# An SSD layer's turnings in one step, and TensorE's order tied once per chunk

## The chip, the cores and the metric

The kernel runs on one core of a Trainium2 chip. The metric is device time in microseconds (us) of one execution; the kernel before took 1810.02 us in the median of three runs (1809.37 to 1811.35). The core's engines are TensorE (PE in the profile, PEld for its weight loads), VectorE (DVE), ScalarE (ACT), GpSimd (POOL) and SyncE (SP, which issues most of the DMAs).

## The reference

Two layers over 256 context rows and 1024 latent rows of width 1024. Layer 0 is gated windowed attention, layer 1 a gated bidirectional Mamba-2 SSD mixer, and a final RMSNorm follows. The change touches layer 1 alone. Cut to it:

```python
z, xbc, dt_raw = jnp.split(h @ w_in, [SSD_WIDTH, SSD_WIDTH + SSD_CONV_DIM], axis=-1)
xbc = jax.nn.silu(centred_depthwise_conv(xbc, conv_w, conv_b))       # 5 taps
xs, bm, cm = jnp.split(xbc, [SSD_WIDTH, SSD_WIDTH + SSD_GROUPS * SSD_STATE], axis=-1)
# per direction, over chunks of 128 rows, per group g (8), head r (4 a group), width 64, state 128
states = jnp.einsum('bcsgn,bcsgr,bcsgrp->bcgrpn', bm, decay_to_end, xdt)
h = exp(a_last) * h + states                                         # scan over the chunks
cb = jnp.einsum('bcqgn,bcsgn->bcqsg', cm, bm)
y_diag = jnp.einsum('bcqsg,bcqsgr,bcsgrp->bcqgrp', cb, lmat, xdt)
y_off = jnp.einsum('bcqgn,bcgrpn,bcqgr->bcqgrp', cm, h_prev, jnp.exp(a_cs))
u = (y_f + y_b + d_skip * xs) * jax.nn.silu(z)                       # forward and backward
out = (rms_normalize(u) * norm_w) @ w_out
```

## The kernel before, in words

**Groups and chunks.** Layer 1 works group by group (8 groups, one for every 256 columns of the mixer). A group needs four projected tiles of 128 channels (B in `bT`, two x tiles in `cacc`, C in `cT`) and the gate z. Each product is split in three (high by high, high by low, low by high). `front(g)` is a generator that gives out the projections of group g one matmul at a time, with an estimated cost each: 24 matmuls of 256 columns for the context (L1085, into the PSUM tile `psD`, of which there is one buffer), 48 of 512 columns for the latent rows (L1095, into `pj2`, two buffers), and for z 192 of 256 columns (L1129, into `pj2` too). After a tile's projections ScalarE takes the first tap (L1007), VectorE the other four (L1011), then the silu (L1018, L1019).

**Turnings.** B and x are needed with rows on the partitions too. `natural` (L1053) turns a tile back in blocks of 128 columns: TensorE writes the turned blocks over the projection's own PSUM tile (L1058), and ScalarE copies them out (L1061): two copies of 512 columns for the latent rows, one of 256 for the context, which sits in `psD`. These steps go to a queue, `post`, with a delay (`LATE`), and are recorded when the estimated cost given out has passed it.

**The scan.** `slot` is one chunk of one group: it opens with the matmul of C and B (`pcb`, L1247), the two products with the states (`po`, L1249 with the forward state, L1250 with the backward one), then the step of the forward state (`S`, L1256), the product within the chunk (`yd`, four matmuls at L1281) and, for the chunk before, the turning of the result (`tail`, two at L1312). These five PSUM tiles share `psX`, three buffers. VectorE, GpSimd and ScalarE make the decay matrix, the sums and the norm between them. `states` runs the chain of backward states of the next group, one link at a time (L1198, into the same `psD` as the context's projections): GpSimd weights x (L1173, `xw`) and decays the state (L1178), VectorE adds (L1210).

**How they are woven.** While group g is scanned, `slot` calls `fill(0)` to `fill(4)` between its parts; each draws projections of group g+1 (in the last group: the output projection, `ssd_out`, L1527) from the generator up to a share of the total, and runs `post` for what was given out; `tick` draws a link of `states`. So the code's order is fixed by estimated costs. It is not yet the engines' order: the framework's scheduler lays the recorded instructions out again, engine by engine, by priority in the order of recording and by when it reckons their inputs and buffers ready. An engine then works its list strictly in order, and a matmul that waits holds up those behind it. In the scheduled order of before, projections stand between the opening's parts, and turnings stand in fours. The second four of a tile (L1058) wait for the copy of the first four (L1061).

## Time and profile before

| | us |
|---|---|
| median of three runs | 1810.02 |
| the profiled execution, its own time | 1807.02 |
| its span, first to last instruction | 1805.3 |
| TensorE matmul busy | 1739.6 (96%) |
| VectorE / ScalarE / GpSimd busy | 1181.8 / 867.1 / 799.0 |
| first opening of a chunk (L1247) to the last | 849.3 to 1674.8 |
| time from a group's first opening to the next group's, groups 1 to 2 | 105.8 |

The page gives each engine's busy time and the costliest groups of instructions with the idle time ahead of them and what ended it ("<-"). A timeline lists instructions by start; "x4" are four merged ones, and the bracket behind a row is the engine's idle time before it. An fp32 matmul that is not a turning leaves two records. Rows of a stretch ("A:B") give the busy time of PE, PEld, DVE, ACT and POOL with the number of instructions, the granted TensorE clock, and the DMA's share and rate.

### The profile page before, as it was taken

How to read it: one execution, taken by the hardware profiler on the slowest of the kernel's cores; microseconds unless marked ns; L12 is line 12 of the kernel's file. 1: busy time of each engine (PE TensorE's matmuls, PEld its weight loads, DVE VectorE, ACT ScalarE, POOL GpSimd, SP SyncE). 2: the span in 40 equal slices, each digit the busy share in tenths (PEclk: the TensorE clock that was granted, in tenths of full speed). 3: DMA queues.
4: the chain of work that ended last, by engine and by line, in shares of the span. 5: the costliest groups of instructions: out<-in, count | busy, mean ns of one | idle time of the engine just before them, and what ended most of it. 6: DMA issues, size and time to landing. Idle time of an engine off the chain costs nothing.

```text
span 1805.3 us, 28983 instructions
## 1 busy us (share of the span) xinstructions
PE 1739.6 (96%) x10319; PEld 1494.7 (83%) x10319; DVE 1181.8 (65%) x2115; ACT 867.1 (48%) x1906; POOL 799.0 (44%) x1068
## 2 busy tenths in 40 slices
PE   6899999999999999999999999999999999999997
PEld 2697788888888887778888898988889898888887
DVE  4634436778877885684776858577684867766734
ACT  3612237777777774452443525344353534544522
POOL 2331127555575545103454544645454464554411
PEclk9999999999999999999999999999999999999999
DMA  9558856444455436222222323222332322656533
GB/s 334 226 144 268 283 177 149 106 100 111 111 153 130 120 102 221 73 53 73 71 77 82 92 62 98 79 71 79 81 93 62 100 73 76 174 169 170 175 101 121
DMA packets 212495, 227.61 MB, mean 126 GB/s; under 512 B 16384, under 2 KB 149632, under 8 KB 212352
## 3 DMA queue, kind: packets, MB, share of 16 engines
q1 hardware_dynamic: 178288, 207.12, 38.0%
q0 software_dynamic: 34064, 18.65, 5.8%
q8 instruction: 81, 1.33, 0.3%
q14 instruction: 62, 0.51, 0.1%
HBM read 190.88 MB, written 35.13 MB: 125 GB/s over the span
## 4 chain that ended last, share of the span: by engine, by line
PE 81%; DVE 9%; ACT 4%; DMA 3%; issue 2%; SPq 1%; POOL 1%; DVEq 0%; ACTq 0%; POOLq 0%
PE pj L1095 17%; PE pj L1129 10%; PE pj L1527 7%; PE pj L246 6%; PE pj L247 6%; PE pj L248 6%; PE psD L1085 4%; PE psX L1281 3%; PE pt L684 3%; PE psD L1198 2%; PE pv L691 2%; PE pv L690 1%; PE S L659 1%; PE S L658 1%; PE psX L1249 1%
## 5 line engine op out<-in xcount | busy, mean ns | idle before, releaser
L246 PE MATMUL pj<-uH,wh 128*128 128x512 f32 (+1 forms) x712 | 257.4, 363 | 9.0 <-ACT uH L470 6.3
L247 PE MATMUL pj<-uL,wh 128*128 128x512 f32 (+1 forms) x712 | 243.3, 342 | 0.5 <-POOL uL L707 0.4
L248 PE MATMUL pj<-uH,wl 128*128 128x512 f32 (+1 forms) x712 | 242.4, 341 | 1.4 <-POOL wl L231 1.4
L1095 PE MATMUL pj<-uH,wl 128*128 128x512 f32 x512 | 172.7, 405 | 0.0
L1095 PE MATMUL pj<-uH,wh 128*128 128x512 f32 x512 | 171.4, 405 | 1.2 <-ACT bn L1061 0.7
L1095 PE MATMUL pj<-uL,wh 128*128 128x512 f32 x512 | 169.2, 402 | 0.0
L246 PEld LDWEIGHTS pj<-uH,wh 128*128 128x128 f32 x712 | 135.6, 191 | 36.2 <-ACT uH L470 7.7
L1129 PE MATMUL pj<-wh,uH 128*128 128x256 f32 x512 | 150.3, 294 | 9.1 <-ACT xn L1061 9.1
L1173 POOL TENSOR_TENSOR xw<-xn,dtdec 128x256 f32<-128x256 f32 x144 | 92.9, 650 | 141.6 <-PE psD L1198 107.1
L1129 PE MATMUL pj<-wh,uL 128*128 128x256 f32 x512 | 152.7, 298 | 0.0
L248 PEld LDWEIGHTS pj<-uH,wl 128*128 128x128 f32 x712 | 135.0, 190 | 18.6 <-POOL wl L231 2.3
L247 PEld LDWEIGHTS pj<-uL,wh 128*128 128x128 f32 x712 | 135.8, 191 | 16.0 <-issue 3.0
L1129 PE MATMUL pj<-wl,uH 128*128 128x256 f32 x512 | 146.7, 287 | 0.0
L689 DVE TENSOR_TENSOR pl<-pt,ph 128x512 fp32r<-128x512 f32 x168 | 114.1, 688 | 47.2 <-ACT ph L688 46.2
L231 POOL TENSOR_TENSOR wl<-wr,wh 128x512 fp32r<-128x512 f32 x76 | 100.2, 1322 | 86.1 <-ACT wh L229 85.2
L663 DVE CUSTOM_DVE_ANT_0 sm<-S,mask,nsink 128x640 f32<-128x640 f32 (+2 forms) x160 | 119.2, 773 | 19.8 <-PE S L659 12.6
L665 ACT ACTIVATE sm<-sm,nm 128x640 f32<-128x640 f32 (+2 forms) x160 | 118.6, 742 | 16.6 <-DVE nm L663 15.9
L688 ACT CAST ph<-pt 128x512 fp32r<-128x512 f32 x168 | 97.5, 586 | 56.0 <-PE pt L684 52.7
L229 ACT CAST wh<-wr 128x512 fp32r<-128x512 f32 (+1 forms) x116 | 74.7, 648 | 87.7 <-PE pj L247 63.5
L1095 PEld LDWEIGHTS pj<-uH,wl 128*128 128x128 f32 x512 | 95.3, 188 | 19.2
L1095 PEld LDWEIGHTS pj<-uL,wh 128*128 128x128 f32 x512 | 95.4, 188 | 18.7
L1129 PEld LDWEIGHTS pj<-wh,uH 128*128 128x128 f32 x512 | 98.7, 193 | 13.5 <-ACT xn L1061 12.1
(339 smaller groups left out, 4810.8 us busy)
## 6 DMA issues: line engine op xcount, KB each, us to landing
wr<-w_x SPq DMA_DIRECT2D x32, 512.0 KB, 4.6
M<-acs SPq DMA_DIRECT2D x64, 256.0 KB, 4.9
bw<-acs SPq DMA_DIRECT2D x64, 256.0 KB, 5.5
wr<-w_sk SPq DMA_DIRECT2D x24, 512.0 KB, 3.8
wr<-wg SPq DMA_DIRECT2D x40, 256.0 KB, 4.5
qs<-q POOLq DMA_DIRECT2D x40, 256.0 KB, 3.9
wada<-w_ada SPq DMA_DIRECT2D x16, 512.0 KB, 7.2
wr<-wq SPq DMA_DIRECT2D x32, 256.0 KB, 3.0
```

The source lines that it names most:

```text
L231: (eng or nc.vector).tensor_tensor(l, raw, h, op=ALU.subtract)
L246: self.nc.tensor.matmul(ps, lh, rh, start=first and i == 0, stop=False)
L247: self.nc.tensor.matmul(ps, lh, rl, start=False, stop=False)
L248: self.last_mm = self.nc.tensor.matmul(ps, ll, rh, start=False, stop=last and i == n - 1)
L663: nc.vector.tensor_tensor_reduce(out=sm[:, :W], in0=Sv, in1=self.mask[:, m0 : m0 + W], scale=-SCALE, scalar=self.nsink[:, 4 * j + r : 4 * ...
L665: nc.scalar.activation(sm[:, :W], sm[:, :W], AF.Exp, bias=nm[:, r : r + 1], scale=-1.0, accum_out=sums[:, r : r + 1])
L688: nc.scalar.copy(ph, ptf)
L689: nc.vector.tensor_sub(pl, ptf, ph)
L1095: nc.tensor.matmul(raw[:, 512 * i : 512 * i + 512], l[:, k, :], r[i][:, k, :], start=k + y == 0, stop=k == KT - 1 and y == 2)
L1129: nc.tensor.matmul(pj[:, c], l, r[:, k, :], start=c % 2 + q + k + y == 0, stop=c % 2 == 1 and q == 1 and k == 3 and y == 2)
L1173: nc.gpsimd.tensor_tensor(xw, X(st, c).rearrange("p (r h) -> p r h", r=R), self.dtdec[:, c, hd(d, g)].unsqueeze(2).broadcast_to([P, R, HP] ...
L1527: nc.tensor.matmul(banks[x], l[:, z, sl], r, start=k == 2 * qs[0] and y == 0, stop=k == 2 * qs[-1] + 1 and y == 2)
```

## The change

Two edits. First, `natural` records all turnings of a tile in one step, and then the copies; before, each copy's turnings stood right ahead of it, so that the second four stood behind the first copy. Second, the order on TensorE is tied. `issue_after(x)` gives each instruction that is recorded inside it, on the engine of x, a tie: it must stand behind x in that engine's list; no semaphore is added. The opening's first matmul must stand behind the last projection that was given out (`self.pe`), and all that a `fill` gives out behind the opening's last matmul (`self.opened`, the product with the backward state). The `post` steps that run in a `fill`, the turnings among them, are inside the tie too. `S`, `yd`, `tail` and the links of `states` are not tied.

```diff
         def natural(raw, acc, dst, o, n):
-            steps = []
-
-            def tr(lo, hi):
-                for x in range(lo, hi):
+
+            def tr():
+                for x in range(n):
                     nc.tensor.transpose(raw[:, x * P : (x + 1) * P], acc[:, x * P : (x + 1) * P], self.ident)
...
-            for d, lo, hi in dst:
-                steps.append(lambda lo=lo, hi=hi: tr(lo, hi))
-                steps.append(lambda d=d, lo=lo, hi=hi: ev(d, lo, hi))
-            return [(LATE, steps)]
+            return [(LATE, [tr] + [lambda d=d, lo=lo, hi=hi: ev(d, lo, hi) for d, lo, hi in dst])]
...
-                        nc.tensor.matmul(raw, l[:, k, :], r[2][:, k, :], start=k + y == 0, stop=k == KT - 1 and y == 2)
+                        self.pe = nc.tensor.matmul(raw, l[:, k, :], r[2][:, k, :], start=k + y == 0, stop=k == KT - 1 and y == 2)
...
-            nc.tensor.matmul(pcb, st["bT"][:, cs], st["cT"][:, cs], start=True, stop=True)
+            with self.tc.issue_after(self.pe.ins):
+                nc.tensor.matmul(pcb, st["bT"][:, cs], st["cT"][:, cs], start=True, stop=True)
             po = t(ps, [P, 512], F32, "psX")
             nc.tensor.matmul(po[:, :256], st["cT"][:, cs], flat(st["hf"]), start=True, stop=True)
-            nc.tensor.matmul(po[:, 256:], st["cT"][:, cs], flat(st["hb"][c]), start=True, stop=True)
+            self.opened = nc.tensor.matmul(po[:, 256:], st["cT"][:, cs], flat(st["hb"][c]), start=True, stop=True)
...
                 def run(until):
                     nonlocal spent
                     while spent < until:
-                        cost = next(work, None)
-                        if cost is None:
-                            return
-                        spent += cost
-                        post.run(cost)
+                        with self.tc.issue_after(self.opened.ins):
+                            cost = next(work, None)
+                            if cost is None:
+                                return
+                            spent += cost
+                            post.run(cost)
```

`self.pe` is set in the same way at the latent projections, at z and in the output projection. The number of instructions of every kind stays as it was. In the changed kernel the lines are numbered anew: L1081, L1091 and L1125 are the projections (before: L1085, L1095, L1129), L1057 the turnings (L1058), L1060 their copies (L1061), L1244, L1246 and L1247 the opening (L1247, L1249, L1250), L1253 `S`, L1278 `yd`, L1309 `tail`, L1194 `states`.

**Place 1: the context's turnings and the next context projections.** TensorE's list before, in the scan of the second group, from the two turnings of the first x tile's context part (`cctx`, into `psD`) to the next projections that need `psD`:

```order
L1058 MATMUL psD_10873<-ident_63,cctx_10910 128x128 x2
L1095 MATMUL pj_2526_11107<-uH_2132_8670,wh_10994 128x512
L1095 MATMUL pj_2526_11107<-uL_2035_8171,wh_10994 128x512
L1095 MATMUL pj_2526_11107<-uL_2133_8671,wh_10994 128x512
L1095 MATMUL pj_2526_11107<-uH_2034_8170,wl_10996 128x512
L1247 MATMUL psX_11182<-cT_10161,bT_9663 128x128
L1095 MATMUL pj_2526_11107<-uH_2132_8670,wl_10996 128x512
L1249 MATMUL psX_11184<-hf_11061,cT_10161 128x256
L1250 MATMUL psX_11184<-hb_2407_10409,cT_10161 128x256
L1312 MATMUL psX_11093<-ident_63,y_2155_8749 128x128
L1058 MATMUL pj_2492_10911<-ident_63,cacc_10912 128x128 x4
L1085 MATMUL psD_11038<-uH_1654_6747,wh_10994 128x256
```

Between the two turnings and the next user of `psD` stand five projections, an opening, a tail and four turnings. TensorE's list now, from the last three projections of that x tile on:

```order
L1091 MATMUL pj_2492_10911<-uL_2133_8671,wh_10798 128x512
L1091 MATMUL pj_2492_10911<-uH_2034_8170,wl_10800 128x512
L1091 MATMUL pj_2492_10911<-uH_2132_8670,wl_10800 128x512
L1309 MATMUL psX_10978<-ident_63,y_2156_8751 128x128
L1057 MATMUL pj_2467_10746<-ident_63,bT_10747 128x128 x8
L1057 MATMUL psD_10873<-ident_63,cctx_10910 128x128 x2
L1081 MATMUL psD_11038<-uH_1654_6747,wh_10994 128x256
L1081 MATMUL psD_11038<-uL_1655_6748,wh_10994 128x256
```

The eight turnings of B and the two of the context now stand together behind the x tile's last projection, and the next context projections, which write the one `psD`, follow at once. ScalarE's list now at the same place (`M` is the decay matrix's exponentials, `wh` a weight's high part, `cacc` the first tap, `uT` the tail's copy, then the copies of the turned tile):

```order
L1232 ACTIVATE M_10857<-M_10857,vf_8731 128x128 x4
L1292 ACTIVATE y_2499_10953,ss_11005<-y_2155_8749 128x257
L1034 CAST wh_11169<-wr_11036 128x1024
L1007 ACTIVATE cacc_10912<-pj_2492_10911,cb_8724,cw_8721 128x1024
L1310 ACTIVATE uT_10979<-psX_10978,nw_8727 128x128
L1060 COPY bn_2455_10692<-pj_2467_10746 128x512
L1060 COPY bn_2456_10693<-pj_2467_10746 128x512
L1060 COPY xn_2454_10691<-psD_10873 128x2x128
```

The copy that frees `psD` (the last row) stands behind a weight, a tap, a tail's copy and both copies of B.

**Place 2: the second x tile's turnings and the first z projections.** Both need the same `pj2` buffer. TensorE's list before:

```order
L1247 MATMUL psX_11464<-cT_10161,bT_9663 128x128
L1058 MATMUL pj_2526_11107<-ident_63,cacc_11108 128x128 x4
L1249 MATMUL psX_11466<-hf_11314,cT_10161 128x256
L1250 MATMUL psX_11466<-hb_2395_10350,cT_10161 128x256
L1198 MATMUL psD_11301<-xw_11284,bn_2457_10694 128x256
L1312 MATMUL psX_11347<-ident_63,y_2155_8749 128x128
L1129 MATMUL pj_2582_11401<-wh_11295,uH_2034_8170 128x256
```

and now:

```order
L1057 MATMUL pj_2526_11107<-ident_63,cacc_11108 128x128 x8
L1309 MATMUL psX_11347<-ident_63,y_2155_8749 128x128
L1194 MATMUL psD_11365<-xw_11326,bn_2457_10694 128x256
L1091 MATMUL pj_2548_11244<-uH_2034_8170,wl_11171 128x512
L1091 MATMUL pj_2548_11244<-uH_2132_8670,wl_11171 128x512
L1125 MATMUL pj_2582_11401<-wh_11295,uH_2034_8170 128x256
```

Before, the second four turnings stood five matmuls ahead of z; now all eight do, with a tail, a link of `states` and two projections between. ScalarE's list now at this place:

```order
L1034 CAST wh_11410<-wr_11399 128x1024
L1232 ACTIVATE M_11231<-M_11231,vf_8731 128x128 x4
L1060 COPY xn_2452_10689<-pj_2526_11107 128x4x128
L1060 COPY xn_2453_10690<-pj_2526_11107 128x4x128
L1310 ACTIVATE uT_11348<-psX_11347,nw_8727 128x128
```

The two copies stand together behind a weight and the four exponentials, where before the second copy stood behind a weight, a tap and a square.

**Place 3: the first chunk of the first scanned group.** TensorE's list now, from the opening on:

```order
L1244 MATMUL psX_9601<-cT_9227,bT_8798 128x128
L1246 MATMUL psX_9603<-hf_2218_9297,cT_9227 128x256
L1194 MATMUL psD_9464<-xw_9441,bn_2161_8760 128x256
L1253 MATMUL psX_9607<-xw_9487,bn_2161_8760 128x256
L1278 MATMUL psX_9644<-xn_2158_8757,M_9099 128x64 x4
L1194 MATMUL psD_9489<-xw_9462,bn_2161_8760 128x256
L1247 MATMUL psX_9603<-hb_2251_9491,cT_9227 128x256
L1081 MATMUL psD_9622<-uH_1654_6747,wh_9539 128x256
```

The opening's last matmul (L1247) waits for the end of the chain of `states`, and no projection may stand ahead of it; before, 13, 22 and 13 projections stood ahead of the first link, between the links, and ahead of L1250.

More of the change, by code (lines that the diff above doesn't have):

```diff
@@ L1094, in front @@
                         for i in q:
-                            nc.tensor.matmul(raw[:, 512 * i : 512 * i + 512], l[:, k, :], r[i][:, k, :], start=k + y == 0, stop=k == KT - 1 and y == 2)
+                            self.pe = nc.tensor.matmul(raw[:, 512 * i : 512 * i + 512], l[:, k, :], r[i][:, k, :], start=k + y == 0, stop=k == KT - 1 and y == 2)
                             yield N512
@@ L1127, in front @@
                         for y, (l, r) in enumerate(((u, ww["h"]), (u, ww["l"]), (v, ww["h"]))):
-                            nc.tensor.matmul(pj[:, c], l, r[:, k, :], start=c % 2 + q + k + y == 0, stop=c % 2 == 1 and q == 1 and k == 3 and y == 2)
+                            self.pe = nc.tensor.matmul(pj[:, c], l, r[:, k, :], start=c % 2 + q + k + y == 0, stop=c % 2 == 1 and q == 1 and k == 3 and y == 2)
                             yield N256
@@ L1526, in ssd_out @@
                         for y, (l, r) in enumerate(((w["h"], hi), (w["h"], lo), (w["l"], hi))):
-                            nc.tensor.matmul(banks[x], l[:, z, sl], r, start=k == 2 * qs[0] and y == 0, stop=k == 2 * qs[-1] + 1 and y == 2)
+                            self.pe = nc.tensor.matmul(banks[x], l[:, z, sl], r, start=k == 2 * qs[0] and y == 0, stop=k == 2 * qs[-1] + 1 and y == 2)
                             yield N512
```

## The prediction

> **What bounds the kernel now.** I read the page's totals first, then the stretches of 100 us, then TensorE's groups inside the scan, then the timeline at the waits. The totals:
>
> ```profile
> span 1805.3 us, 28983 instructions
> PE 1739.6 (96%) x10319; PEld 1494.7 (83%) x10319; DVE 1181.8 (65%) x2115; ACT 867.1 (48%) x1906; POOL 799.0 (44%) x1068
> PE 81%; DVE 9%; ACT 4%; DMA 3%; issue 2%; SPq 1%; POOL 1%; DVEq 0%; ACTq 0%; POOLq 0%
> ```
>
> TensorE is the bound, and the chain that ended last is 81% TensorE. In the scan (849 to 1675 us) a stretch of 100 us looks like this:
>
> ```profile
> 1100.00:1200.00 100.00, 98.69 (x610) 88.13 (x608) 67.14 (x116) 42.16 (x100) 49.46 (x69) 1.00 0.30 79
> ```
>
> TensorE works 98.7 of 100 us at the full clock (1.00), so the change can win about 1.3 us in 100. Who holds that little? One wait, of z on a copy of turned blocks:
>
> ```profile
> PE pj L1129 <- ACT xn L1061: 9.1, 7, 1.3
> ```
>
> It is 9.1 us in 7 places, 1.3 us each, once a group. No other wait of a matmul over 0.15 us lies between 849 and 1590 us. The work itself stays: the same instructions are on TensorE before and after. So the question is only which waits the new order takes away and which it makes.
>
> **What a wait of this kind is made of.** The one at 1029 us in the timeline, ScalarE and TensorE:
>
> ```profile
> 1027.04 0.35 ACT L1313 ACTIVATE uT<-psX,nw 128x128 f32<-128x128 f32 x1
> 1027.04 0.60 PE L1058 MATMUL pj<-ident,cacc 128*128 128x128 f32 x4
> 1027.29 1.03 ACT L1034 CAST wh<-wr 128x1024 fp32r<-128x1024 f32 x1
> 1028.22 1.20 ACT L1007 ACTIVATE cT<-pj,cb,cw 128x1024 f32<-128x1024 f32 x1
> 1029.33 0.41 ACT L1295 ACTIVATE y<-y 128x257 f32<-128x257 f32 x1
> 1029.72 0.57 ACT L1061 COPY xn<-pj 128x512 f32<-128x512 f32 x1
> 1030.19 0.38 ACT L1202 COPY hx<-psD 128x256 f32<-128x256 f32 x1
> 1030.35 0.39 PE L1129 MATMUL pj<-wh,uH 128*128 128x256 f32 x1 [1.30 <-ACT xn L1061]
> ```
>
> The reader is to see that ScalarE is not busy on average (42 of 100 us) and yet holds TensorE, since the copy stands behind a tail's copy, a weight and a tap. Start to start these cost 0.25, 0.93 and 1.11 us, and a copy of 512 columns 0.47. TensorE goes on 0.06 us behind the copy's end (1029.72 + 0.57 = 1030.29), and its first matmul takes 0.11 us more than the 0.28 of its like: 0.17 together.
>
> **Part 1, a new wait at place 1.** Before, the same two context turnings (`psD`) have cover:
>
> ```profile
> 1197.83 0.38 PE L1058 MATMUL psD<-ident,cctx 128*128 128x128 f32 x2
> 1198.04 0.27 PE L1312 MATMUL psX<-ident,y 128*128 128x128 f32 x1
> 1198.15 0.60 PE L1249 MATMUL psX<-hf,cT 128*128 128x256 f32 x2
> 1198.59 0.59 PE L1250 MATMUL psX<-hb,cT 128*128 128x256 f32 x2
> 1199.02 0.60 PE L1058 MATMUL pj<-ident,bT 128*128 128x128 f32 x4
> 1199.45 0.60 PE L1256 MATMUL psX<-xw,bn 128*128 128x256 f32 x2
> 1200.03 1.10 PE L1281 MATMUL psX<-xn,M 128*128 128x64 f32 x8
> 1200.95 0.36 PE L1085 MATMUL psD<-uH,wh 128*128 128x256 f32 x1
> ```
>
> From the turnings to the context projections that need `psD` again lie 3.1 us of other matmuls, so the copy is hidden and L1085 waits for nothing. In the new list nothing lies between. I count from the start of the x tile's last projection. TensorE: that projection 0.23, a tail 0.11 (1198.04 to 1198.15), eight turnings at 0.108 (four took 1199.02 to 1199.45) 0.86, two more 0.22: the context could start at 1.42 us. ScalarE: the weight's high part needs the buffer that the third projection from the end reads; that one starts at -0.46, and a 512-column matmul's record lasts 0.39, so the cast starts at about -0.03. Then by the pitches above: weight 0.93, tap 1.11, tail's copy 0.25, two copies of 0.47, and the copy of 256 columns 0.36, by this row:
>
> ```profile
> 1006.60 0.36 ACT L1061 COPY xn<-psD 128x256 f32<-128x256 f32 x1
> ```
>
> This is 3.59, so `psD` is free at 3.56, and with the 0.17 of the restart TensorE goes on at 3.73: a wait of 2.3 us. Ahead of the weight stand the four exponentials and a square; those took
>
> ```profile
> 1025.85 1.28 ACT L1236 ACTIVATE M<-M,vf 128x128 f32<-128x128 f32 x4
> ```
>
> 1.28 and 0.41 us, and whether they are done in time hangs on the chain over VectorE and GpSimd. Were they to start only then, the wait would be 4.0; were weight, tap and tail's copy all out of the way, three copies would be left: 0.47 + 0.47 + 0.36 + 0.17, less the 0.22 of TensorE's two turnings, 1.25 us. I take 2.5, near the list as it stands with a little of the exponentials in the way. It comes once a group, 7 times: **+17.5 us** (9 to 28). Queued behind it are the opening, `S` and `yd` of the next chunk; all of TensorE's list moves by it.
>
> **Part 2, the wait at place 2.** z now waits for two copies that follow eight turnings, with cover of a tail (0.11), a link (0.43, as L1249 above to L1250) and two projections (0.46): 1.0 us. The copies with an idle ScalarE take 0.04 + 0.47 + 0.57 + 0.17 = 1.25, a wait of 0.25; with the exponentials running 0.5 us past the turnings, 0.75. I take 0.5, between the two, in place of 1.3: 7 x -0.8 = **-5.6 us** (-9.1 to 0).
>
> **Part 3, the opening at place 3.** Before, the last two links have long cover:
>
> ```profile
> 852.92 0.59 PE L1198 MATMUL psD<-xw,bn 128*128 128x256 f32 x2
> 853.59 0.62 POOL L1173 TENSOR_TENSOR xw<-xn,dtdec 128x256 f32<-128x256 f32 x1
> 853.62 0.42 DVE L1210 TENSOR_TENSOR hb<-hb,psD 128x256 f32<-128x256 f32 x1 [0.58 <-PE psD L1198]
> 863.10 0.59 PE L1250 MATMUL psX<-hb,cT 128*128 128x256 f32 x2
> ```
>
> Between the link at 852.92 and L1250 TensorE had 10 us of projections to do, which may not stand there now. `S` needs an `xw` that GpSimd starts at 0.67 behind the link's start and ends at 1.29; with 0.17 of restart that is 1.46, and TensorE reaches it after 0.43: a wait of 1.0. L1250 needs the second link's addition, which ends 1.12 behind its start; 1.29 against 0.43 is a wait of 0.9. About 2 us, once. In the last group the list has the same `S` behind a link and then output projections behind L1250: 1 us more. In the groups between, eight z projections, two parts of the opening and `S` (2.0 us) follow the last link, more than the 1.3 it needs: 0. Sum **+3 us** (0 to 4).
>
> **Costed at nothing.** Turnings in one step: in the scan the second four never waited long (no row), and ahead of the scan the waits between the fours, 1.09 us at most, become one wait for both copies. SyncE's and GpSimd's lists shift with the rest, but the DMA share in the scan is 0.30 and no matmul there waits for a transfer: what hides them is that slack, and without it each late load would be a wait of the weight's high part at place 1. Fewer changes between projections and scan matmuls on TensorE (38 rows fewer in its list): nothing, since the scan's matmuls at 1198 us keep their pitch of 0.43 us among other kinds as in a row.
>
> **Sum.** 17.5 - 5.6 + 3 = 14.9. Against the profiled execution's own 1807.02 (span 1805.3) this is 1821.9; its three timed runs have the median 1810.02, 3.0 above it, so I expect 1824.9: **1825 us**, 0.8% slower.
>
> **Rivals.** *The clock.* The trace shows once what a pause of TensorE does to its clock, ahead of the scan:
>
> ```profile
> 780.62:784.03 3.41, 1.80 (x12) 1.10 (x10) 3.41 (x6) 2.63 (x3) 0.00 (x0) 1.00 0.00 0
> 811.34:814.75 3.41, 3.41 (x17) 2.56 (x15) 0.00 (x0) 0.49 (x1) 0.78 (x1) 1.00 0.68 179
> 814.75:818.17 3.42, 0.81 (x6) 0.45 (x5) 2.09 (x4) 2.30 (x6) 0.95 (x3) 1.00 0.58 105
> 818.17:825.00 6.83, 6.22 (x23) 4.96 (x24) 6.55 (x6) 2.61 (x5) 3.12 (x5) 0.50 0.60 192
> 825.00:828.40 3.40, 3.40 (x29) 3.35 (x29) 1.32 (x2) 1.40 (x2) 0.79 (x2) 1.00 0.00 0
> ```
>
> After 3.42 us with 0.81 us of matmul records, the granted clock was 0.50 for 6.83 us, which loses 3.4 us; after 3.41 us with 1.80 us it stayed. At place 1 a tail, ten turnings and the wait make a stretch of 3.7 us without a projection, with about 1.3 us of records in it: between the two. If some of the 7 places fall so, 1 to 5 times 3.4 us come on top: 1828 to 1842. I give 30%. [...]
>
> *Faster.* ScalarE is idle more than half the time. If it ran so far ahead at place 1 that only a sliver of the wait were left, z's 9.1 us would be the whole effect: 1807.0 - 9.1 + 3.0 + 7 waits of at most 0.5 = 1801 to 1804. It decides at 0.78 us of wait a group (9.1 less 0.2% of the time, by 7), with nothing lost at place 3. Against it stands the 1.25 that three copies need with all else gone. 8%.
>
> *The change does little.* The floor of 1.25 at place 1 (+8.8), z's wait all gone (-9.1), and place 3 hidden: within 0.2%, or 3.6 us, which is about what a measurement can tell from no change. 7%.
>
> *Longer.* The exponentials come late each time, 4.0 us at place 1: 10.5 us more, 1835. 5%.
>
> **Chances.** Forecast (1817 to 1831) 50%, clock 30%, longer 5%, little 7%, faster 8%. Slower is the sum of the first three, 85%. The range leaves out the faster case, most of "little" and the far end of the clock: 1814 to 1838.
>
> **What would show it.** Right: L1081 with about 17 us of idle time in 7 places ended by ScalarE's L1060; L1125's 9.1 down to 2 to 5; two waits of about 1 us near the first opening; stretches of 100 us with TensorE at 97 rather than 98.7. The clock: stretches in the scan with a granted clock under 1.00. Wrong: no wait at L1081, or waits at the opening (L1247) or `yd` in each group, which I put at nothing.

## The result and the profile after

The changed kernel took **1834.13 us** in the median of four runs (1832.84 to 1834.65), the kernel before 1809.69 us beside it: a ratio of 1.0132 (95% interval 1.0115 to 1.0149), slower. The profiled execution took 1832.84 us. Its page, the totals and the chain that ended last:

```profile
span 1831.1 us, 28963 instructions
PE 1745.7 (95%) x10319; PEld 1501.8 (82%) x10319; DVE 1182.7 (65%) x2115; ACT 869.9 (48%) x1906; POOL 793.1 (43%) x1068
PE 77%; DVE 10%; ACT 5%; DMA 3%; issue 3%; POOL 2%; SPq 1%; DVEq 0%; ACTq 0%; POOLq 0%
```

The number of matmuls is the same, TensorE's busy time grew by 6.1 us, the span by 25.8. So most of the loss is idle time of TensorE, and some of it is the same work at a slower pace. The chain names who is waited for: VectorE, ScalarE and GpSimd hold 17% of it now, 14% before. TensorE's waits of the changed kernel (us in total, times, longest):

```profile
PE psD L1081 <- ACT xn L1060: 19.2, 8, 2.6
PE psD L1194 <- POOL xw L1169: 5.4, 1, 5.4
PE pj L1125 <- ACT xn L1060: 5.1, 8, 0.7
PE psX L1247 <- DVE hb L1206: 1.5, 1, 1.5
PE psX L1278 <- ACT uH L1483: 0.8, 1, 0.8
PE psX L1253 <- POOL xw L1169: 0.8, 1, 0.8
```

The first row is place 1: one of the eight lies ahead of the scan (1.1 us), the other seven are 2.58 to 2.59 us each, once a group, 18.1 us. The second row lies ahead of the scan. The third is z at place 2: seven waits of 0.67 to 0.70 us, 4.8, and one ahead of the scan; they were 1.3 each. The fourth and the last are place 3; the fifth is `yd` in the last group. One of the seven at place 1, on ScalarE and TensorE:

```profile
994.57 0.68 ACT L1232 ACTIVATE M<-M,vf 128x128 f32<-128x128 f32 x2
...
995.15 0.41 ACT L1292 ACTIVATE y<-y 128x257 f32<-128x257 f32 x1
...
995.38 1.04 PE L1057 MATMUL pj<-ident,bT 128*128 128x128 f32 x8
...
995.55 1.03 ACT L1034 CAST wh<-wr 128x1024 fp32r<-128x1024 f32 x1
...
996.25 0.38 PE L1057 MATMUL psD<-ident,cctx 128*128 128x128 f32 x2
996.49 1.20 ACT L1007 ACTIVATE cacc<-pj,cb,cw 128x1024 f32<-128x1024 f32 x1
...
997.59 0.35 ACT L1310 ACTIVATE uT<-psX,nw 128x128 f32<-128x128 f32 x1
...
997.84 1.05 ACT L1060 COPY bn<-pj 128x512 f32<-128x512 f32 x2
998.78 0.38 ACT L1060 COPY xn<-psD 128x256 f32<-128x256 f32 x1
...
999.22 0.39 PE L1081 MATMUL psD<-uH,wh 128*128 128x256 f32 x1 [2.58 <-ACT xn L1060]
```

The reader is to see ScalarE's list as the prediction wrote it down, without a gap: weight, tap, tail's copy, both copies of B, and last the copy that frees `psD`.

But the waits alone are not the 25.8 us. A stretch of 100 us in the scan (busy us of PE, PEld, DVE, ACT, POOL; granted clock; DMA share and rate):

```profile
1100.00:1200.00 100.00, 96.71 (x607) 87.18 (x606) 63.70 (x110) 43.07 (x100) 48.50 (x69) 0.98 0.32 75
```

TensorE works 96.7 of 100 us instead of 98.7, and the granted clock is 0.98 instead of 1.00. The clock's records show where: it is 0.50 for 3.4 us at 999.9, 1109.2, 1218.4, 1327.6, 1436.9 and 1546.1 us, right behind six of the seven waits. Stretches of 3.41 us laid along these edges, around the first wait (ended at 891.57) and the second (ended at 999.22):

```profile
887.26:890.67 3.41, 1.73 (x14) 1.36 (x12) 1.69 (x2) 3.41 (x9) 0.55 (x1) 1.00 0.45 100
890.67:894.09 3.42, 2.52 (x16) 2.36 (x17) 3.28 (x6) 1.26 (x4) 0.00 (x0) 1.00 0.76 200
...
996.49:999.90 3.41, 0.82 (x7) 0.68 (x6) 3.25 (x3) 3.08 (x7) 0.00 (x0) 1.00 0.50 90
999.90:1003.31 3.41, 3.41 (x13) 2.87 (x12) 3.37 (x6) 0.00 (x0) 0.00 (x0) 0.51 0.42 145
```

Both waits last 2.58 us. The first is shared by two windows, with 1.73 and 2.52 us of matmul records in them, and nothing follows. The second lies whole in one window, 0.82 us of records are left in it, and the next window runs at 0.51: 3.41 us of time for 1.7 us of work, so 1.7 us lost (the product with the forward state, L1246, takes 1.06 us there at 1000.50, and 0.60 at 892.61 at the full clock). Six times, that is 10 us. That all six fall alike follows from the length of a group: from edge to edge it is 109.2 us, 32 times the 3.413 us that each of these six halvings lasts, and a group with its halving takes 109.3, so the wait moves by only 0.1 us a group against the windows.

**The sum of it.** From the first opening of one group to that of the next:

| us | 1 to 2 | 2 to 3 | 3 to 4 | 4 to 5 | 5 to 6 | 6 to 7 | 7 to 8 | sum |
|---|---|---|---|---|---|---|---|---|
| before | 105.47 | 105.77 | 105.78 | 105.78 | 105.77 | 105.79 | 105.35 | 739.7 |
| changed | 111.02 | 109.33 | 109.39 | 109.30 | 109.35 | 109.29 | 108.86 | 766.5 |

These seven steps hold 26.8 us, more than the whole difference of 25.8; ahead of the first opening it is -0.7, behind the last one of the table -0.3. Their terms: place 1 +18.1, z 4.8 - 9.1 = -4.3, the opening at place 3 0.75 + 1.47 = +2.2, the clock 6 x 1.7 = +10.2, together 26.2. What is left is 0.6: the first step alone holds 1.4 us that none of these terms names, the others each 0.1 to 0.2 less than theirs. Of the 1.4, 0.9 are two links of `states` that now fall into this step (26 matmul records for 22, 0.43 us a link), where before they fell into the last group; the rest I have not traced.

### The profile page after: what moved, and what is told of

Its sections match the earlier page's. It is cut to its first block, busy times and chain, and to the rows that moved or that the text cites. A ratio compares the mean times of both kernels' runs of the same rounds, so it can differ in the third digit from the quotient of the medians.

```text
span 1831.1 us, 28963 instructions
## 1 busy us (share of the span) xinstructions
PE 1745.7 (95%) x10319; PEld 1501.8 (82%) x10319; DVE 1182.7 (65%) x2115; ACT 869.9 (48%) x1906; POOL 793.1 (43%) x1068
## 4 chain that ended last, share of the span: by engine, by line
PE 77%; DVE 10%; ACT 5%; DMA 3%; issue 3%; POOL 2%; SPq 1%; DVEq 0%; ACTq 0%; POOLq 0%
PE pj L1091 16%; PE pj L1125 9%; PE pj L1525 7%; PE pj L246 6%; PE pj L247 6%; PE pj L248 6%; PE psD L1081 4%; PE pt L684 3%; PE psX L1278 3%; PE pv L691 2%; PE psX L1247 2%; PE psD L1194 2%; PE psX L1246 2%; PE pv L690 1%; PE S L659 1%
## 5 line engine op out<-in xcount | busy, mean ns | idle before, releaser
L1169 POOL TENSOR_TENSOR xw<-xn,dtdec 128x256 f32<-128x256 f32 x144 | 93.5, 650 | 218.9 <-PE psX L1253 120.2
L1091 PE MATMUL pj<-uH,wh 128*128 128x512 f32 x512 | 170.0, 403 | 1.8 <-ACT bn L1060 1.2
L1091 PE MATMUL pj<-uH,wl 128*128 128x512 f32 x512 | 169.6, 405 | 0.0
L1091 PE MATMUL pj<-uL,wh 128*128 128x512 f32 x512 | 166.6, 398 | 0.0
L246 PEld LDWEIGHTS pj<-uH,wh 128*128 128x128 f32 x712 | 135.6, 191 | 33.8 <-issue 6.4
L1125 PE MATMUL pj<-wh,uH 128*128 128x256 f32 x512 | 150.1, 293 | 5.1 <-ACT xn L1060 5.1
L1125 PE MATMUL pj<-wh,uL 128*128 128x256 f32 x512 | 152.9, 299 | 0.0
L1125 PE MATMUL pj<-wl,uH 128*128 128x256 f32 x512 | 150.1, 293 | 0.0
L1091 PEld LDWEIGHTS pj<-uL,wh 128*128 128x128 f32 x512 | 96.3, 188 | 20.0
L1091 PEld LDWEIGHTS pj<-uH,wl 128*128 128x128 f32 x512 | 96.3, 188 | 19.1
L1091 PEld LDWEIGHTS pj<-uH,wh 128*128 128x128 f32 x512 | 93.7, 188 | 19.9 <-ACT bn L1060 1.4
```

What stands on the lines that cost most here:

```text
L246: self.nc.tensor.matmul(ps, lh, rh, start=first and i == 0, stop=False)
L1091: self.pe = nc.tensor.matmul(raw[:, 512 * i : 512 * i + 512], l[:, k, :], r[i][:, k, :], start=k + y == 0, stop=k == KT - 1 and y == 2)
L1125: self.pe = nc.tensor.matmul(pj[:, c], l, r[:, k, :], start=c % 2 + q + k + y == 0, stop=c % 2 == 1 and q == 1 and k == 3 and y == 2)
L1169: nc.gpsimd.tensor_tensor(xw, X(st, c).rearrange("p (r h) -> p r h", r=R), self.dtdec[:, c, hd(d, g)].unsqueeze(2).broadcast_to([P, R, HP] ...
```

## The experiments

Each kernel was run beside the kernel before on the same chip, so the ratios are the safest numbers. The profiled executions differ in one more thing: the first context projection, ahead of which all these kernels are alike, starts anywhere from 746.3 to 756.7 us. Stretches counted from there are free of that:

| kernel | median, us | ratio to before (95%) | first context projection to first opening | first to last opening | first context projection to end | clock at 0.50 in the scan |
|---|---|---|---|---|---|---|
| before | 1809.69 | | 101.4 | 825.5 | 1057.5 | 0 |
| changed | 1834.13 | 1.0132 (1.0115 to 1.0149) | 102.3 | 847.4 | 1084.9 | 20.5 |
| 1 no opening tie | 1811.95 | 1.0009 (0.9996 to 1.0022) | 103.1 | 823.7 | 1061.8 | 0 |
| 2 own tile | 1814.91 | 1.0033 (1.0019 to 1.0046) | 102.1 | 826.7 | 1063.8 | 0 |
| 3 filled wait | 1831.49 | 1.0110 (1.0079 to 1.0140) | 102.9 | 844.2 | 1082.2 | 6.8 |
| 4 turnings only | 1826.64 | 1.0086 (1.0057 to 1.0114) | 102.6 | 857.5 | 1079.7 | 20.5 |
| 5 ties only | 1858.10 | 1.0279 (1.0250 to 1.0309) | 101.7 | 872.3 | 1109.0 | 47.8 |
| 6 no fill tie | 1833.44 | 1.0142 (1.0116 to 1.0168) | 102.4 | 863.0 | 1082.2 | 17.1 |
| 7 own tile, no ties | 1800.18 | 0.9958 (0.9941 to 0.9974) | 102.7 | 811.9 | 1050.0 | 0 |
| 8 own tile, opening tie | 1803.21 | 0.9964 (0.9952 to 0.9976) | 102.6 | 813.7 | 1050.0 | 0 |
| 9 shifted wait | 1842.19 | 1.0176 (1.0154 to 1.0199) | 102.7 | 850.2 | 1087.6 | 17.1 |
| 10 own tile in before | 1806.68 | 0.9994 (0.9979 to 1.0009) | 101.2 | 825.3 | 1056.4 | 0 |
| 11 as 7, fours ahead of the scan | 1797.85 | 0.9940 (0.9920 to 0.9961) | 101.0 | 810.4 | 1046.6 | 0 |

Theory: the loss is the wait for `psD` at place 1 and the halved clock behind it. The rivals: the wait would only move on to the next matmul, the clock has another cause, or the turnings in one step lose by themselves.

### 1. Without the opening's tie

```diff
-            with self.tc.issue_after(self.pe.ins):
+            if True:
                 nc.tensor.matmul(pcb, st["bT"][:, cs], st["cT"][:, cs], start=True, stop=True)
```

> The changed kernel without one of its two ties: the opening's first matmul need no longer stand behind the last projection. Theory A (the loss sits in the wait of the context projections for psD, 2.6 us in 7 places, and in the six halvings of the clock behind it, and the opening's tie makes that wait because it takes the opening, S and yd out from between the context's turnings and the next context projections): those three stand there again, the wait goes, the clock stays at 1.00, and the time is near the kernel before, 1806 to 1814 us. z then waits about 1.2 us again, 7 times. Rival B (the eight turnings in one step make the wait, whatever stands between): L1081 still waits 7 times about 2 us, 1825 to 1834 us. Rival C (the tie of the fills makes it): also 1825 to 1834 us, with the wait at L1081 unchanged.

1811.95 us, a ratio of 1.0009: the whole loss is gone. TensorE's waits on ScalarE, and a stretch of the scan:

```profile
PE pj L1125 <- ACT xn L1060: 7.2, 7, 1.2
...
PE psD L1081 <- ACT xn L1060: 1.1, 1, 1.1
```

```profile
1100.00:1200.00 100.00, 98.85 (x622) 88.88 (x621) 68.10 (x115) 43.38 (x102) 49.75 (x70) 1.00 0.34 84
```

The one wait left at L1081 is the one ahead of the scan; z waits 1.15 us in six of the seven groups, nearly as before (1.3), and the clock is 1.00. As theory A has it; B and C fall, since both the one-step turnings and the tie of the fills are still there.

### 2. The turned context blocks in a tile of their own

```diff
+            box = {0: raw}
             def tr():
+                if n == 2 and g:
+                    box[0] = t(ps, [P, 512], F32, "psX")
                 for x in range(n):
-                    nc.tensor.transpose(raw[:, x * P : (x + 1) * P], acc[:, x * P : (x + 1) * P], self.ident)
+                    nc.tensor.transpose(box[0][:, x * P : (x + 1) * P], acc[:, x * P : (x + 1) * P], self.ident)
...
-                nc.scalar.copy(d[:, :, o : o + P], raw[:, lo * P : hi * P].rearrange("p (c n) -> p c n", n=P))
+                nc.scalar.copy(d[:, :, o : o + P], box[0][:, lo * P : hi * P].rearrange("p (c n) -> p c n", n=P))
```

> The changed kernel, but the two turned blocks of a context tile are written to a tile of psX of their own instead of over the projection's psD (from the second group on), so that psD comes free when VectorE has read it and not when ScalarE has copied the turned blocks. All turnings, copies and ties stay. Theory A (wait for the copy plus clock): the wait at L1081 goes, 7 x 2.6 = 18 us; no halving, 6 x 1.7 = 10 us; some of it comes back as waits of the opening or of the products for a buffer of psX, at most 1.5 us a group: 1806 to 1818 us, and no granted clock of 0.50 between 900 and 1600 us. Rival B (ScalarE as such is late at this place, and holds whatever comes next): the wait only moves to the opening (L1249 or so) at 2 us or more in each group, and the time stays over 1825 us. Rival C (the halvings belong to the bulk of ten turnings, not to the wait): six halvings stay, 1816 to 1828 us.

1814.91 us, 19.2 under the changed kernel. The context projections are L1085 here, the opening L1250, z L1129:

```profile
PE psX L1250 <- ACT uT L1314: 6.2, 7, 0.9
...
PE pj L1129 <- ACT xn L1064: 4.1, 8, 0.5
...
PE psD L1085 <- ACT xn L1064: 1.1, 1, 1.1
```

The wait for `psD` is gone from the scan and the halvings with it, though all ties stand. Some of it comes back as the opening's wait for a `psX` buffer, 0.88 us in 7 groups, within theory A's bound of 1.5 and far from B's 2. Rival C falls too: the ten turnings still stand together, and no clock record under 1.00 is in the scan. (The schedule also moved: `yd`, 1.0 us, now stands between the turnings and the context projections, less than the 2.58 that had been waited.)

### 3. Work put into the wait

```diff
                 raw = t(ps, [P, 512], F32, "psD")[:, :CTX]
+                if n == 2 and g:
+                    idle = t(ps, [P, 512], F32, "psX")
+                    for e in range(6):
+                        nc.tensor.matmul(idle, wh[:, e % KT, :], uH[0][:, e % KT, :], start=True, stop=True)
```

> The changed kernel with 6 matmuls of 512 columns more in each of the 7 groups, into a spare tile of psX that nobody reads, recorded ahead of the second x tile's context projections; in TensorE's list they stand just ahead of the ten turnings. They add 6 x 0.23 = 1.4 us of work a group, nearly all of which fits into the wait at L1081, which should fall from 2.6 to 1.2 to 1.8 us. Theory A1 (the six halvings come from too little matmul work around the wait): with the added work there is none, and although work is added the time falls by some 6 to 10 us, to 1824 to 1829 us. Theory A2 (the halvings have another cause, and the loss is the wait alone): six halvings of 3.4 us stay, and the time is the same or up to 4 us more, 1833 to 1839 us.

1831.49 us, with an interval that takes in the changed kernel's ratio: by the time alone this decides nothing. The trace does. Waits, with L1085 for the context projections and L1282 for `yd`:

```profile
PE psD L1085 <- ACT xn L1060: 12.5, 8, 1.6
...
PE psX L1282 <- DVE dg L1267: 1.9, 1, 1.9
```

and the two windows at the wait that ended at 1003.65, then what the turnings (L1057) have in the first of them, whose columns are PE and PEld alone:

```profile
1000.41:1003.82 3.41, 1.79 (x14) 1.43 (x13) 3.12 (x3) 3.19 (x7) 0.00 (x0) 1.00 0.54 88
1003.82:1007.23 3.41, 3.41 (x25) 3.26 (x26) 3.37 (x7) 0.00 (x0) 0.65 (x2) 1.00 0.43 156
```

```profile
1000.41:1003.82 3.41, 1.25 (x10) 1.12 (x10) 1.00 0.54 88
```

There are 1.79 us of records in the window instead of 0.82, and the next one stays at 1.00; in none of the seven groups is the wait, 1.62 us now, followed by a halving. A group takes 108.03 to 108.05 us in four of the inner ones: against 109.33 it has 1.38 us more work and 0.97 less wait, so 109.74 were to be expected with the clock as it was, and 1.7 us are missing, the price of one halving. This shows A1's cause. Its time was off: 1831.5 lies 2.5 us above its range. The six more matmuls a group cost 2.9 us net, and in the last group `yd` waits 1.9 instead of 0.8, behind which the clock is halved once, for 6.8 us.

### 4. The turnings alone, no ties

```diff
-            for d, lo, hi in dst:
-                steps.append(lambda lo=lo, hi=hi: tr(lo, hi))
-                steps.append(lambda d=d, lo=lo, hi=hi: ev(d, lo, hi))
-            return [(LATE, steps)]
+            return [(LATE, [tr] + [lambda d=d, lo=lo, hi=hi: ev(d, lo, hi) for d, lo, hi in dst])]
```

> The kernel before with the first edit alone: all turnings of a tile in one step, no ties. Theory A (the ties make the loss): in the second and third group other matmuls stand between the context's turnings and the next context projections, so that there is no wait of 2 us in each group; z's wait of 1.3 us shrinks too; the order drifts in later groups and may bring waits of its own at the links of the states: 1800 to 1820 us, no regular halving. Rival B (the turnings in one step make the loss): L1081 waits over 2 us 7 times, 1825 us or more.

1826.64 us, above the 1800 to 1820 that I had put down: a miss in size. The scan has two halves:

```profile
855.00:955.00 100.00, 100.00 (x629) 90.48 (x628) 70.01 (x118) 43.35 (x101) 52.23 (x71) 1.00 0.32 78
1500.00:1600.00 100.00, 93.53 (x576) 83.32 (x575) 68.34 (x113) 47.22 (x103) 42.26 (x58) 0.96 0.45 133
```

Four steps from group to group take 103.7 to 104.3 us, with TensorE hardly idle, and the next three 114.8, 108.3 and 116.0. What waits there are the links of `states` (L1194):

```profile
PE psD L1194 <- DVE hb L1206: 5.7, 4, 2.6
...
PE psD L1194 <- ACT hx L1198: 4.8, 2, 2.9
```

and the clock is halved for 20.5 us behind them and one `yd`. So B is out (L1081 doesn't wait in the scan), but the first edit is neither free nor harmless: it takes z's wait away, and then TensorE's scheduled order drifts.

### 5. The ties alone, turnings in fours

```diff
-            return [(LATE, [tr] + [lambda d=d, lo=lo, hi=hi: ev(d, lo, hi) for d, lo, hi in dst])]
+            for d, lo, hi in dst:
+                steps.append(lambda lo=lo, hi=hi: tr(lo, hi))
+                steps.append(lambda d=d, lo=lo, hi=hi: ev(d, lo, hi))
+            return [(LATE, steps)]
```

> The changed kernel without the first edit: the ties stay, but the turnings of a tile stand in fours again, each copy behind its own four. Theory A (the ties and the one-step turnings must go together): the second four of a tile now wait right behind the first four for ScalarE's copy, about 2 us twice a group, z waits about 1.5 us, and the context projections nothing, since the context's turnings stand between the fours: about 4 to 5 us a group in place of 1.3 before, 1829 to 1845 us, and halvings of the clock where a wait of 2 us stands beside turnings. Rival B (the ten turnings in one step alone fed the wait at L1085): without them the ties cost little, 1808 to 1820 us.

1858.10 us, the slowest, and 13 us above theory A's range. Here L1058 are the turnings, L1129 z and L1198 the links:

```profile
PE pj L1058 <- ACT bn L1061: 13.9, 8, 2.3
...
PE pj L1058 <- ACT xn L1061: 8.4, 8, 2.2
PE psD L1198 <- ACT hx L1202: 8.2, 3, 2.7
...
PE pj L1129 <- ACT xn L1061: 6.3, 4, 1.6
```

The waits are those of theory A, and a link's wait besides; the clock, halved for 47.8 us with 44.4 us of matmul records in them, takes some 22 more, which I had named but not priced. So the second four of a tile, tied to the fills, are left without cover; the first edit mends that, and the change as a whole is 24 us better than its second edit alone.

### 6. Without the tie of the fills

```diff
-                        with self.tc.issue_after(self.opened.ins):
+                        if True:
                             cost = next(work, None)
```

> The changed kernel without the tie of the fills; the opening's tie stays. Theory A (the tie of the fills keeps the groups alike; without it TensorE's order drifts from group to group as with the first edit alone, which took 103.8 us a group for four groups and then 108 to 116): group times that differ by several us, waits at the links of the states or at latent projections in the later groups, no wait of 2.6 us in each group, 1815 to 1830 us. Rival B (the opening's tie alone makes the wait of 2.6 us): the wait at L1081 stays in most of the groups, with halvings, 1828 to 1836 us.

1833.44 us, as slow as the changed kernel, but otherwise: the steps from group to group are 103.8, 104.2, 104.7, 105.9, 115.1, 108.5 and 114.7, the drift of experiment 4.

```profile
PE pj L1091 <- DVE wl L1038: 5.4, 5, 2.0
PE psD L1194 <- ACT hx L1198: 3.7, 2, 2.5
PE psD L1081 <- ACT xn L1060: 2.1, 2, 1.1
```

No wait of 2.6 us a group, so the opening's tie alone does not make it (rival B falls, and with it the half of my theory that blamed this tie alone). With experiment 1: the wait at place 1 needs both ties and the one-step turnings. Theory A's mechanism holds, its 1815 to 1830 is missed by 3 us.

### 7 and 8. The own tile without the ties, and with the opening's tie

Experiment 7 is the edit of experiment 2 on the kernel of experiment 4; experiment 8 is the changed kernel with the edits of experiments 2 and 6.

> Turnings in one step, the turned context blocks in a psX tile of their own, no ties. Theory A (what stands between 105.8 and 103.8 us a group is z's wait and small ones, and the drift of the first edit alone begins where psD is contended between the context and the links of the states): with psD freed early the order stays without large waits in all groups, 103.7 to 105 us each, 1797 to 1806 us. Rival B (the drift has to do with the missing ties, not with psD): waits of 1 to 3 us at the links in the fifth to seventh group as with the first edit alone, 1810 to 1828 us.

> The changed kernel with a psX tile of its own for the turned context blocks, and without the tie of the fills (the opening's tie stays). Theory A (the opening's tie costs nothing once psD does not wait for ScalarE, and the tie of the fills costs the opening at place 3 and the 0.9 us a group at L1250): 104 to 105.5 us a group, 1799 to 1808 us, faster than both kernels or equal to the faster one. Rival B (without the tie of the fills the order drifts): groups of 108 us and more, 1812 to 1828 us.

1800.18 and 1803.21 us, both faster than both kernels. A stretch of the scan of experiment 7, where experiment 4 had 93.5:

```profile
1500.00:1600.00 100.00, 100.00 (x622) 89.88 (x621) 79.59 (x131) 50.41 (x109) 54.41 (x73) 1.00 0.53 153
```

The last four steps from group to group take 104.0 us each in experiment 7, 104.2 in 8. The drift is gone without a tie: it hung on `psD`, which the context shares with the links, or on what an earlier `psD` does to the scheduled order; the two I can't tell apart. The ties bring nothing that the own tile doesn't.

### 9. The wait moved against the windows

```diff
+                if i == 1 and q == 0 and g:
+                    idle = t(ps, [P, 512], F32, "psX")
+                    for e in range(6):
+                        nc.tensor.matmul(idle[:, :256], uH[0][:, e, :P], ww["h"][:, e % 4, :], start=True, stop=True)
                 if i == 1 and q == 0 and g + 1 < G:
```

> The changed kernel with 6 matmuls of 256 columns more in the middle of each group's z projections, into a spare tile of psX that nobody reads: 0.7 to 1.2 us of work more a group, far from the wait at L1081, which stays at 2.6 us in 7 places. In the changed kernel the halvings follow windows of 3.413 us: the wait that lies whole in one window (0.82 us of matmul records in it) is followed by 3.4 us at 0.50, the first one, which two windows share (1.73 and 2.52 us of records), is not; and a group there takes 109.2 us, 32 windows, so that each wait falls like the one before. Theory A (the place of the wait in the window decides): a group of another length moves the waits through the windows, 1 to 4 of the 7 are halved instead of 6, each with under 1.7 us of records in its window, and in spite of 5 to 8 us more work the time stays within 3 us of the changed kernel: 1831 to 1837 us. Theory B (each wait of this length is halved, the first was an exception for another reason): 6 or 7 halvings, 1839 to 1843 us.

1842.19 us and five halvings: between the theories in the count, and with B in the time. Which of the waits were halved speaks for A. The windows of the second wait, and of the fourth:

```profile
1003.39:1006.80 3.41, 1.06 (x10) 0.82 (x8) 2.36 (x2) 3.41 (x7) 0.55 (x1) 1.00 0.36 90
1006.80:1010.21 3.41, 3.17 (x12) 2.91 (x13) 2.40 (x6) 0.59 (x2) 0.00 (x0) 0.50 0.63 190
...
1221.81:1225.23 3.42, 1.71 (x14) 1.34 (x12) 1.73 (x2) 3.42 (x9) 0.55 (x1) 1.00 0.39 111
1225.23:1228.64 3.41, 2.54 (x16) 2.39 (x17) 3.34 (x4) 1.23 (x4) 0.00 (x0) 1.00 0.77 191
```

The fourth wait, 2.58 us like the others, is no first one, lies across two windows, and is not halved. But I had expected the waits to run through the windows, and they did not: three of the five steps with a halving came out at 109.2 us again, since z's wait of 0.7 us is missing there. From the first context projection to the end it is 2.8 us more than the changed kernel, with some 5 us of work added; the rest of the 9.5 us between the two profiled executions lies ahead of that projection (753.0 against 746.3 us), where nothing was edited. The experiment supports the place in the window (1.06 us of records were followed by 0.50, 1.71 by 1.00), and says little on the time.

### 10. The own tile in the kernel before

The edit of experiment 2 in the kernel before: turnings in fours, no ties.

> The kernel before with nothing changed but that the two turned blocks of a context tile go to a psX tile of their own (from the second group on); turnings in fours, no ties. Theory A (the gain of the kernel with own tile and one-step turnings comes from the first edit, which takes z's wait of 1.3 us a group away, and the own tile only keeps the first edit's order from drifting): waits of some 0.3 to 0.5 us at the opening and at z instead of z's 1.3, 105.5 to 106 us a group, 1805 to 1814 us. Theory B (the own tile by itself makes the gain): 104 us a group, 1797 to 1803 us.

1806.68 us, a ratio of 0.9994: no change. The inner steps take 105.1 us, 0.4 under my bound, but of the 3.4 us that the seven steps win the last group gives 2.7 back. So the gain of experiment 7 needs the first edit with the own tile; theory B falls. In the last group an output projection waits 1.8 us; the window that holds this wait, and the next:

```profile
1597.13:1600.54 3.41, 1.61 (x9) 1.02 (x7) 3.41 (x5) 3.13 (x9) 2.59 (x3) 1.00 0.82 219
1600.54:1603.96 3.42, 3.42 (x15) 2.84 (x16) 3.42 (x7) 0.00 (x0) 0.97 (x2) 1.00 0.47 142
```

The first has 1.61 us of matmul records, and the second stays at 1.00.

### 11. Fours ahead of the scan

The kernel of experiment 7, with this in `natural`:

```diff
+            if g == 0:
+                steps = []
+                for d, lo, hi in dst:
+                    steps.append(lambda lo=lo, hi=hi: tr(lo, hi))
+                    steps.append(lambda d=d, lo=lo, hi=hi: ev(d, lo, hi))
+                return [(LATE, steps)]
```

> One-step turnings and an own psX tile for the turned context blocks, no ties, as in the kernel that took 1800 us, but ahead of the scan (group 0) the turnings stand in fours as before. Theory A (ahead of the scan the one-step turnings cost: a link of the states now waits 5.4 us where the waits were 2.3, 0.3 and 0.6 us, and about 1 us of that is not given back): the link's wait falls to about 0.3 us with 2.3 and 0.6 at the turnings, the first opening comes 1 to 2 us earlier after the first context projection, and the time is 1797 to 1801 us. Theory B (the wait is only idle time that the halved clock at that place would have wasted anyway): the same time as that kernel, within 1 us in the stretch up to the first opening.

1797.85 us, the fastest version here. From the first context projection to the first opening it is 101.0 us instead of 102.7 in experiment 7, theory A. The waits there (L1061 turnings, L1204 the link):

```profile
PE pj L1061 <- DVE cacc L1019: 1.6, 1, 1.6
...
PE pj L1061 <- ACT xn L1064: 1.1, 1, 1.1
...
PE psD L1204 <- POOL xw L1179: 0.3, 1, 0.3
```

The link's wait of 5.5 us went, as expected; the turnings wait 1.6 and 1.1 where 2.3 and 0.6 were expected. TensorE's idle time in that stretch fell by 3.3 us (9.2 to 5.9), but its matmul records grew by 1.6, since the clock's two halved windows now hold 6.6 us of records and not 4.2; so 1.7 came out. Against experiment 7 the times alone (intervals 0.9920 to 0.9961 and 0.9941 to 0.9974) don't separate the two.

## Why the prediction was right, and where it missed

The forecast was 1825 us in a range of 1814 to 1838; it is 1834. Slower was right, for the reason given, and the forecast was 9 us low by one term.

- **Part 1, right.** Predicted 2.5 us in 7 places, 17.5; measured 2.58 to 2.59, 18.1. The list gave 2.3, and it was off where the text said it might be: the weight's high part started at 995.55, about 0.5 us later than the list had it, behind the exponentials and the square. From there on the pitches hold: 0.94, 1.10, 0.25, and 0.94 for the two copies of B. Experiments 1 and 2 show it as the cause: with the wait taken away in two different ways 1.6 and 6.0 us of it are left (by the ratios 1.0009 and 1.0033).
- **Part 2, right.** 0.5 us taken, 0.69 measured: -4.3 for -5.6.
- **Part 3, right in kind.** `S` waits 0.75 (1.0) and L1247 1.47 (0.9), 2.2 us for 1.9; in the last group it is `yd` (L1278, 0.8) and not `S`.
- **"Costed at nothing", wrong by 1 to 2 us.** Ahead of the scan I wrote that the waits between the fours "become one wait for both copies". For B they did (1.09 and 0.67 became 1.16), but a link waits 5.4 us, where before the turnings waited 2.3 and 0.6 and the link 0.3. Part of that was given back (the halved clock there fell on 3.8 us of matmul records, where before it fell on 6.2), and 0.9 us were lost up to the first opening (102.3 for 101.4); experiment 11 got 1.7 back by undoing it.
- **The sum: the step that failed is the clock, kept out of the sum.** The forecast added 17.5 - 5.6 + 3. The rival "The clock" had the missing term, with the right evidence: 1 to 5 places at 3.4 us were given, 6 places at 1.7 came, 10 us. That 1834 lies inside its 1828 to 1842 is in part luck: the price was twice too high, the count too low, and the two offset each other. What I should have asked is how the wait falls into windows. Of the 3.41 us of positions 0.83 hold the wait of 2.58 whole, a quarter, which is an estimate from these two figures; such a window, with 0.82 to 0.84 us of records, was followed by a halving each time. With part of the wait in it, a window of 1.06 us of records was too (experiment 9), and those of 1.61 (experiment 10), 1.71 (experiment 9) and 1.73 (the changed kernel) were not; how many of the positions between bring a halving is not shown. Two things were wrong in the rival's price. A halving lasted one window here, and not two as in the row ahead of the scan; that row was also not the only one, as the prediction has it: the trace of before has a halving of one window at 53.6 us, behind 0.85 us of records, which would have given the price. And I counted the places as independent, where the period of a group, 32 windows and 0.1 us once halved, brings each wait to nearly the same place.
- **Turnings.** In experiment 3's window of 1.79 us of records the turnings had 1.25, the tail 0.27, the added matmuls 0.42 and a context projection 0.17 (records overlap); the last two are 0.59 of other work, and the clock stayed at 1.00. In the changed kernel's window of 0.82 L1081 alone had 0.68, and 0.50 followed. So the other work alone does not tell the two windows apart; what a turning weighs against another matmul the runs do not show.
- **The other rivals.** *Faster* decided at 0.78 us of wait a group, and the wait was 2.58. *Little* and *longer* did not come either: the exponentials were late by half a microsecond, not by all of their time.

What stays open: why the scheduled order drifts in experiments 4 and 6, beyond that it stops with the own tile or the tie of the fills, 0.5 us of the first step from group to group, and what decides on a halving where a window holds between 1.1 and 2.3 us of records.

## What to carry to other kernels

A tie on the order of a saturated engine takes away the cover that a scheduler had put between a release and its next user: before tying, list what stands between each buffer's last reader and its next writer, and count the copying engine's whole list up to the copy, not its busy share. Price an idle stretch of TensorE by what the granted clock does behind it as well as by its length: here a wait of 2.58 us cost 1.7 us more where one window of 3.41 us held it, and nothing more where two shared it. Compare the period of the loop with that window too: here 109.3 us a group, 32 windows and 0.1 us, brought six waits to the bad place. Where a wait is for a buffer that another engine only copies out of, another tile for the copied data can do more than any order: here it made the first edit a gain of 0.6% (0.9940, 0.9920 to 0.9961, with fours ahead of the scan).

## What the runs showed of the hardware

- In the scan of the changed kernel the granted clock was at 0.50 six times, for 3.413 us each, and from one such edge to the next it was 109.2 us, 32 times as long. Ahead of the scan, in the kernel before, it was at 0.50 for 6.83 us at 26.27 and at 818.17, and for 3.41 us at 53.58.
- The six came behind windows with 0.82 to 0.84 us of matmul records; in experiment 9 the windows at 1003.39 and 1112.59, with 1.06 and 1.09 us, were followed by 0.50 too. Windows with 1.61 (experiment 10), 1.71 (experiment 9), 1.73 (the changed kernel) and 1.79 us (experiment 3) were followed by 1.00. These figures are no bound: ahead of the scan of the kernel before, a window with 2.30 us (22.86 to 26.27) was followed by 0.50, and one with 1.80 us (780.62 to 784.03) by 1.00.
- The time lost was half of the work that fell into the halving: 3.41 us of records in the window at 999.90, so 1.7 us, as experiment 3 priced it. Where idle time fell into it, less work was slowed: ahead of the scan 6.83 us at 0.50 held 6.22 us of records in the kernel before and 3.8 in the changed kernel, 3.1 and 1.9 us lost (an estimate, half of each).
- In the changed kernel the groups kept step with the clock's windows: one with a halving took 109.3 us, 32 windows and 0.1 us, and the next wait was halved too, five times in a row (without the 1.7 us of the halving a group would be 107.6, 31.5 windows, an estimate). In experiment 9 the two windows named above lie 109.20 us apart, 32 windows.
- With the same program up to there, the first context projection started from 746.3 to 756.7 us in thirteen profiled executions. Differences of a few us between kernels are better read behind such a point than from the span.
